# A scan's cost on VectorE, doubled in the planner's model that sets the order of issue

## The chip, the cores and the metric

The kernel runs on one core of a Trainium2 chip. The metric is the device time of one execution in microseconds (us). The core has five engines that take their instructions in order from a queue of their own: TensorE (PE, matrix products), VectorE (DVE), ScalarE (ACT), GpSimd (POOL) and SyncE (SP, which starts most transfers). What one engine hands to another passes through semaphores. An instruction that waits holds up all that stand behind it on its engine.

## The reference, cut to what matters

A trunk of two layers over 512 tokens of width 1024, all in float32. Each layer has a mixer part and a feed-forward part (FFN), with a norm around both:

```python
h = rmsnorm(x, g_pre);  p = h @ W_in        # columns go to four mixers
x = x + rmsnorm(concat(A, B, C, D) @ W_out, g_post)
x = x + rmsnorm(swiglu(rmsnorm(x, ...)), ...)
```

Mixer A is gated linear attention (GLA) in chunks, in both directions over the tokens; B a neighbourhood attention; C a recurrence (RG-LRU) in both directions; D a dilated attention. Two of them hold sums along the tokens:

```python
b = jnp.cumsum(log_a, axis=3)                       # A, in each chunk of 64 tokens
att = einsum(q * exp(b - b_mid), k * exp(b_mid - b))    # A, masked, then att @ v
S = S * d_c[..., None] + kv_c                       # A, a state from chunk to chunk
h = linear_scan(a[0], u[0]) + flip(linear_scan(flip(a[1]), flip(u[1])))    # C
```

The kernel does each of these with one VectorE instruction, `tensor_tensor_scan`, which walks along the free dimension: `y[i] = a[i] * y[i-1] + b[i]`.

## The kernel before, in words

All work is cut into Python generators called threads: a weight to be split, a projection, a direction of a mixer, a head of an attention. Each yields the letter of the engine that its next instructions go to (P, A, V, G for TensorE, ScalarE, VectorE, GpSimd, D for transfers; `A:Exp` also names the table of functions that ScalarE must have loaded). The loop `Builder.go` (L357) runs while the program is built, not on the chip. It keeps a model clock for each engine and takes, again and again, the thread that by the model can start first: `key = (s, th.pri, th.seq)`, where `s` is the later of the engine's clock and the time the thread's input is ready, plus a price for a new table (`SWITCH`, 1290 ns). The order in which the threads are taken is the order of instructions in every engine's queue, and it is fixed from then on.

The model's duration of an instruction comes from `Timed` (L153 on), a wrapper around all four engines: its `call` adds an estimate `t` in ns to `self.b.cost` and then issues the instruction at L198. That is why L198 is the line of nearly every instruction in the profile, and why rows are told apart by tiles. For VectorE (`kind == "V"`) the estimate is 70 ns and 1.04 ns for each element of a row, or 0.52 for some.

`tensor_tensor_scan` has three callers, and there are 24 such instructions, 12 in each layer:

- `dir_a` (L1419), one direction `e` of mixer A for a pair of heads, 4 in a layer: the scan over 512 tokens is the sum of log gates, with a tile `rst` of ones and zeros that restarts it (`m<-rst,m`). ScalarE's exponentials of it follow, then VectorE's products with q and k; then the thread starts `att_a` (L1476), whose matrix products (`bx<-m,m 64*128 64x128`, sixteen for a direction) need these, and `state_a`.
- `gate_c` (L1124), 4 in a layer: the recurrence of mixer C over 512 tokens (`m<-m,m`).
- `state_a` (L1493), 4 in a layer: the state of mixer A over 192 elements.

The first two add 70 to the cost by hand.

Two choices are also made by the model's clocks. `copy` (L412) puts the copy of a PSUM bank on ScalarE or VectorE, whichever clock stands lower. `split` (L403) makes the two parts of an operand: ScalarE rounds it to the high part (`wh`, a CAST), and VectorE or, for most weights, VectorE or GpSimd takes the difference as the low part (`wl`). A dense step of TensorE is the six products of high and low parts into one bank of 128x512.

Of the kernel before, what the change touches and what calls it, by code (L numbers as in the profile page):

```python
# [152 lines left out]
class Timed:  # L153
# [5 lines left out]
    def __getattr__(self, name):  # L159
        f = getattr(self.eng, name)  # L160

        def call(out, *a, **k):
            n = 1
            for s in out.shape[1:]:
                n *= s
            kind = self.kind
            src = a[0] if a and not isinstance(a[0], float) else out
            bank = src.tensor.name[:2] in ("bd", "bx")
            aps = sum(not isinstance(v, (int, float, str)) for v in a[1:] + tuple(k.values()) if hasattr(v, "shape"))
            if kind == "P":  # L170
                if name == "transpose":
                    t = 109.0
                else:
                    m = 1
                    for s in a[0].shape[1:]:
                        m *= s
                    t = max(n / 2.4, m / 1.2) + 13
                    if a[0].dtype == F32:
                        t = max(4 * n / 2.4, 2 * m / 1.2) + 6
                        if a[0].shape[0] == 64 or m == 64:  # L180
                            t *= 0.6
            elif kind == "A":
                t = (51 if bank else 94) + n * 0.833
                if name == "activation" and (aps or "accum_out" in k):
                    t += 93
            elif kind == "V":
                fast = name in ("tensor_scalar", "tensor_copy") and not bank
                t = 70 + n * (0.52 if fast else 1.04)
                if name in ("scalar_tensor_tensor", "tensor_scalar") and aps and n > 16:
                    t += 60  # L190
            elif kind == "G":
                t = 110 + n * (3.4 if name == "tensor_copy" else 2.15)
                if ALU.pow in a:
                    t = 300 + 160 * n
            else:
                t = 60
            self.b.cost += t
            return f(out, *a, **k)  # L198

        return call  # L200
# [1776 lines left out]
```

## Time and profile before

| | us |
|---|---|
| median of 3 runs | 1246.41 (1246.25 to 1246.86) |
| the profiled execution | 1245.09 |
| its span in the trace | 1243.3 |
| TensorE busy | 1203.1 (97%) |
| VectorE busy | 883.8 (71%) |
| ScalarE busy | 707.5 (57%) |
| GpSimd busy | 246.7 (20%) |

The span is the time from the first to the last recorded instruction; 1.8 us of the execution lie outside it. Busy time counts what an engine does, not what it waits. [...] In a timeline, what stands in brackets at the end of a row is the idle time of the engine just ahead of it and the engine and tile that ended it.

### The profile page before, as it was taken

To read this page: it belongs to the slowest core of one execution; us is meant where nothing else is said; L and a number is where in the kernel's file an instruction comes from. 1 tells how busy PE (TensorE), PEld (TensorE's weight loads), DVE (VectorE), ACT (ScalarE), POOL (GpSimd) and SP (SyncE) were. 2 spreads that over 40 slices of the span, in tenths; PEclk is the share of its full clock that TensorE was granted. 3 is DMA by queue.
4 is the path that set the end of the run, shared out by engine and by line. 5 is a ranking of instruction groups with operands and counts; after the bars stand their busy time and mean duration, and the time that the engine had idled before them with its cause. 6 is when DMAs were issued, how large, how long until landed. Compare 5 with 4: busy or idle time off the path is not lost.

```text
span 1243.3 us, 21744 instructions
## 1 busy us (share of the span) xinstructions
PE 1203.1 (97%) x7810; PEld 1050.1 (84%) x7810; DVE 883.8 (71%) x1867; ACT 707.5 (57%) x1604; POOL 246.7 (20%) x255
## 2 busy tenths in 40 slices
PE   7999999999999999999999899999999999999997
PEld 7876777789999999778897677677899999997885
DVE  6467674579766778777875766655897767787775
ACT  6476754565544555566658657455654445556561
POOL 5021111133111110412140111112411121104120
PEclk9999999999999999999999899999999999999999
DMA  7523115218677753988550332430377777639771
GB/s 234 180 75 112 34 61 178 85 45 187 165 187 185 184 138 118 221 227 187 170 199 1 119 85 54 151 110 27 89 191 170 175 193 168 145 92 236 203 182 69
DMA packets 93229, 175.09 MB, mean 141 GB/s; under 512 B 10816, under 2 KB 11200, under 8 KB 93120
## 3 DMA queue, kind: packets, MB, share of 16 engines
q1 hardware_dynamic: 72672, 136.46, 34.6%
q0 software_dynamic: 20160, 36.71, 17.8%
q8 instruction: 61, 1.00, 0.3%
q10 hardware_dynamic: 288, 0.52, 0.1%
q14 instruction: 48, 0.39, 0.1%
HBM read 167.36 MB, written 4.19 MB: 138 GB/s over the span
## 4 chain that ended last, share of the span: by engine, by line
PE 76%; issue 7%; DVE 7%; DMA 4%; ACT 4%; POOL 2%; SPq 0%; POOLq 0%; DVEq 0%; ACTq 0%
PE bx L198 40%; PE bd L198 36%; DVE m L198 5%; ACT m L198 3%; DMA m<-in_wf 3%; POOL wl L198 1%; DMA ws<-in_w 1%; ACT wh L198 1%; DVE wl L198 1%; POOL s L198 1%; POOL m L601 0%; DVE s L198 0%; DMA m<-in_w 0%; POOL att L289 0%; DVE sbd L198 0%
## 5 line engine op out<-in xcount | busy, mean ns | idle before, releaser
L198 PE MATMUL bd<-m,wh 128*128 128x256 f32 (+1 forms) x1600 | 358.5, 318 | 3.4 <-DVE bd L198 2.4
L198 PE MATMUL bx<-m,m 128*128 128x256 f32 (+8 forms) x2096 | 334.0, 340 | 9.7 <-DVE m L198 9.0
L198 DVE TENSOR_TENSOR wl<-m,wh 128x512 fp32r<-128x512 f32 x318 | 219.5, 692 | 152.5 <-ACT wh L198 144.9
L198 DVE TENSOR_TENSOR m<-m,m 128x512 fp32r<-128x512 f32 (+3 forms) x551 | 297.1, 571 | 39.5 <-ACT m L198 37.3
L198 PEld LDWEIGHTS bx<-m,m 128*128 128x128 f32 (+2 forms) x2096 | 257.1, 180 | 70.6 <-issue 25.6
L198 ACT CAST wh<-m 128x512 fp32r<-128x512 f32 x342 | 211.1, 619 | 177.3 <-PE bd L198 90.8
L198 PEld LDWEIGHTS bd<-m,wh 128*128 128x128 f32 x1600 | 261.3, 192 | 25.3 <-issue 6.0
L198 PE MATMUL bd<-m,wl 128*128 128x256 f32 (+1 forms) x800 | 251.6, 314 | 0.0
L198 PEld LDWEIGHTS bd<-m,wl 128*128 128x128 f32 x800 | 153.4, 192 | 9.3
L198 ACT ACTIVATE m<-m 128x256 fp32r<-128x256 f32 (+1 forms) x246 | 112.2, 482 | 61.5 <-DVE m L198 54.9
L198 PE MATMUL bx<-m,wh 128*128 128x256 f32 x768 | 142.4, 284 | 1.0 <-ACT bd L198 1.0
L198 PE MATMUL bd<-m,m 128*128 128x256 f32 (+1 forms) x864 | 137.3, 308 | 1.0 <-DVE m L198 1.0
L514 POOL DMA_DIRECT2D m<-in_wf x76 | 66.9, 973 | 306.2 <-DVE m L198 121.4
L198 PEld LDWEIGHTS bd<-m,m 128*128 128x128 f32 x864 | 119.5, 191 | 8.9 <-DVE m L198 1.4
L198 PEld LDWEIGHTS bx<-m,wh 128*128 128x128 f32 x768 | 119.9, 192 | 1.4 <-ACT bd L198 1.4
L198 ACT CAST m<-m 128x512 fp32r<-128x512 f32 x184 | 108.0, 614 | 15.2 <-DVE m L198 12.7
L198 PE MATMUL bx<-m,wl 128*128 128x256 f32 x384 | 108.8, 283 | 0.0
L198 PE MATMUL bx<-wh,m 128*128 128x512 f32 x296 | 105.7, 398 | 1.6 <-ACT wh L198 1.4
L601 POOL DMA_DIRECT2D m<-in_wf x64 | 56.1, 964 | 165.6 <-DVE m L198 115.2
L198 PE MATMUL bd<-wh,m 128*128 128x512 f32 x232 | 80.7, 394 | 0.0
L198 ACT COPY m<-bx 128x512 f32<-128x512 f32 (+2 forms) x88 | 42.3, 494 | 59.3 <-PE bx L198 58.8
L198 PEld LDWEIGHTS bx<-m,wl 128*128 128x128 f32 x384 | 73.8, 192 | 0.0
(110 smaller groups left out, 1260.7 us busy)
## 6 DMA issues: line engine op xcount, KB each, us to landing
m<-in_wf SPq DMA_DIRECT2D x314, 256.0 KB, 4.0
m<-in_wf POOLq DMA_DIRECT2D x140, 256.0 KB, 5.9
m<-in_w SPq DMA_DIRECT2D x66, 256.0 KB, 5.6
ws<-in_w SPq DMA_DIRECT2D x15, 512.0 KB, 3.8
m<-in_wo SPq DMA_DIRECT2D x24, 256.0 KB, 4.1
m<-in_x SPq DMA_DIRECT2D x14, 256.0 KB, 3.8
m<-in_rpb SPq DMA_DIRECT2D x12, 256.0 KB, 3.6
m<-m SPq DMA_DIRECT2D x32, 64.0 KB, 2.0
```

Of the source, the lines that this page charges most:

```text
L198: return f(out, *a, **k)
L514: self.nc.gpsimd.dma_start(q[name], src, accum_op=ALU.add)
L601: self.nc.gpsimd.dma_start(tile, src, accum_op=ALU.add)
```

## The change

In the model's branch for VectorE, a scan gets its own estimate, 80 ns and 2.08 ns for each element:

```diff
             elif kind == "V":
                 fast = name in ("tensor_scalar", "tensor_copy") and not bank
                 t = 70 + n * (0.52 if fast else 1.04)
+                if name == "tensor_tensor_scan":
+                    t = 80 + n * 2.08
                 if name in ("scalar_tensor_tensor", "tensor_scalar") and aps and n > 16:
                     t += 60
```

With the callers' 70, a scan of 512 counts 1215 ns instead of 672, one of 192 counts 479 instead of 270. No instruction's operands or function change; the planner's choices do. The rows below are the program's order on one engine, by the names of the tiles; the numbers in the names run with the program and shift between the two kernels, and after the change the line of the issue is L200.

TensorE in layer 1, around the first direction of mixer A's first pair. `bd_8062` before is `bd_8060` after, a bank of the projection of v; `m_8102,m_8103` before and `m_8099,m_8100` after are the products of exponentials with k and q; `bd_8293` before and `bd_8265` after are the bank of the projection that follows. Before:

```order
L198 MATMUL bd_8062<-wl_8164,m_6210 128x512
L198 MATMUL bd_8062<-wh_8163,m_6218 128x512
L198 MATMUL bx_8267<-m_8102,m_8103 128x128
L198 MATMUL bx_8268<-m_8102,m_8103 128x128
...
L198 MATMUL bx_8063<-wh_8163,m_6210 128x512
L198 MATMUL bx_8063<-wl_8164,m_6210 128x512
...
L198 MATMUL bd_8293<-m_6203,wh_8188 128x512
```

After:

```order
L200 MATMUL bd_8060<-wl_8163,m_6208 128x512
L200 MATMUL bd_8060<-wh_8162,m_6216 128x512
L200 MATMUL bx_8061<-wh_8162,m_6208 128x512
...
L200 MATMUL bd_8265<-m_6201,wh_8182 128x512
...
L200 MATMUL bx_8283<-m_8099,m_8100 128x128
L200 MATMUL bx_8284<-m_8099,m_8100 128x128
...
L200 MATMUL bd_8265<-m_6203,wh_8182 128x512
```

Two dense steps, one into the bank `bx_8061` and the first into `bd_8265`, stand ahead of the sixteen products of mixer A instead of behind them.

VectorE in the same place: `m_8102<-rst,m_8103` is the scan of direction 0 (a scan prints as SCALAR_TENSOR_TENSOR here), `m_8107<-rst,m_8108` that of direction 1, `m_7963<-m_7964,m_7942` a scan of mixer C, `s_8167` the small products that the exponentials wait for. Before:

```order
L198 SCALAR_TENSOR_TENSOR m_8102<-rst,m_8103 128x512
L198 SCALAR_TENSOR_TENSOR m_8108<-bx_8088,m_8107 128x512
L198 TENSOR_SCALAR s_8167<-m_8102 128x4 x2
L198 TENSOR_TENSOR s_8167<-m_8102 128x4
L198 SCALAR_TENSOR_TENSOR m_8107<-rst,m_8108 128x512
L198 TENSOR_TENSOR m_7942<-m_7955,m_7942 128x512
L198 TENSOR_SCALAR s_8181<-m_8107 128x4 x2
L198 TENSOR_TENSOR s_8181<-m_8107 128x4
L198 SCALAR_TENSOR_TENSOR m_7963<-m_7964,m_7942 128x512
L198 TENSOR_TENSOR m_7938<-m_7938,m_7963 128x512
```

After, where `m_8099<-rst,m_8100`, `m_8104<-rst,m_8105`, `m_7961<-m_7962,m_7940` and `s_8165` are the same things:

```order
L200 SCALAR_TENSOR_TENSOR m_8099<-rst,m_8100 128x512
L200 SCALAR_TENSOR_TENSOR m_8105<-bx_8086,m_8104 128x512
L200 TENSOR_TENSOR m_7940<-m_7953,m_7940 128x512
L200 TENSOR_TENSOR wl_8163<-ws_7604,wh_8162 128x512
L200 SCALAR_TENSOR_TENSOR m_7961<-m_7962,m_7940 128x512
L200 TENSOR_SCALAR s_8165<-m_8099 128x4 x2
L200 TENSOR_TENSOR s_8165<-m_8099 128x4
L200 TENSOR_TENSOR m_7936<-m_7936,m_7961 128x512
L200 TENSOR_TENSOR wl_8183<-m_7670,wh_8182 128x512
L200 TENSOR_TENSOR m_7936<-m_7936,m_7969 128x512
L200 SCALAR_TENSOR_TENSOR m_8104<-rst,m_8105 128x512
```

The scan of direction 1 moved behind the whole of mixer C's scan; a gate product of mixer C, a weight split and mixer C's scan moved ahead of direction 0's small products.

TensorE in layer 0, around the same pair: `m_914,m_915` are direction 0's products, `m_919,m_920` direction 1's, `bd_1137` before and `bd_1131`, `bd_1189` after are banks of a projection. Before:

```order
L198 MATMUL bd_1137<-m_133,wh_1087 128x512
L198 MATMUL bd_1137<-m_125,wl_1088 128x512
L198 MATMUL bx_1189<-m_914,m_915 128x128
L198 MATMUL bx_1190<-m_914,m_915 128x128
...
L198 MATMUL bx_1191<-ident,m_915 128x128 x4
L198 MATMUL bx_1208<-m_919,m_920 128x128
...
L198 MATMUL bx_1217<-ident,m_920 128x128 x4
L198 MATMUL bd_1137<-m_126,wh_1087 128x512
```

After:

```order
L200 MATMUL bd_1131<-m_125,wl_1074 128x512
L200 MATMUL bd_1131<-m_126,wh_1073 128x512
...
L200 MATMUL bd_1189<-m_120,wh_1103 128x512
...
L200 MATMUL bd_1189<-m_121,wl_1104 128x512
L200 MATMUL bx_1212<-m_914,m_915 128x128
L200 MATMUL bx_1213<-m_914,m_915 128x128
...
L200 MATMUL bx_1214<-ident,m_915 128x128 x4
L200 MATMUL bx_1228<-m_919,m_920 128x128
```

Here too the first direction's products stand two dense steps further back.

## Rows read from the trace of the kernel before

**Rows 1.** The page's head: the span, and each engine's busy time.

```profile
span 1243.3 us, 21744 instructions
PE 1203.1 (97%) x7810; PEld 1050.1 (84%) x7810; DVE 883.8 (71%) x1867; ACT 707.5 (57%) x1604; POOL 246.7 (20%) x255
```

**Rows 2.** Waits of TensorE: total us, times, longest.

```profile
PE bx L198 <- DVE m L198: 20.0, 19, 4.8
```

**Rows 3.** Windows: length; busy PE, PEld, DVE, ACT, POOL; granted clock; DMA share; GB/s.

```profile
101.10:103.55 2.45, 0.00 (x1) 0.04 (x1) 2.04 (x4) 2.45 (x8) 0.00 (x0) 1.00 0.11 25
696.20:701.10 4.90, 0.06 (x3) 0.04 (x2) 3.83 (x7) 3.78 (x13) 0.00 (x1) 0.90 0.95 325
701.10:706.90 5.80, 5.80 (x25) 4.81 (x26) 2.53 (x5) 1.90 (x6) 1.57 (x1) 0.50 0.51 191
706.90:765.00 58.10, 58.10 (x347) 43.45 (x347) 35.96 (x83) 36.06 (x75) 9.29 (x6) 1.00 0.23 63
765.00:800.00 35.00, 34.15 (x226) 24.09 (x225) 27.00 (x63) 19.05 (x50) 5.85 (x4) 1.00 0.30 92
```

**Rows 4.** VectorE's groups by shape: busy us, mean ns of one.

```profile
L198 DVE COPY m<-bx 128x512 f32<-128x512 f32 x20 | 13.3, 684 | 7.0 <-PE bx L198 7.0
L198 DVE TENSOR_TENSOR_SCAN m<-rst,m 128x512 f32<-128x512 f32 x8 | 10.7, 1345 | 0.0
L198 DVE TENSOR_TENSOR_SCAN m<-m,m 128x512 f32<-128x512 f32 x8 | 9.5, 1210 | 0.0
L198 DVE TENSOR_TENSOR_SCAN m<-m 128x192 f32<-128x192 f32 x8 | 4.8, 608 | 0.2
```

**Rows 5.** TensorE's timeline in layer 1: start, us, instruction, idle before.

```profile
692.01 0.39 PE L198 MATMUL bd<-wh,m 128*128 128x512 f32 x1
...
693.37 0.39 PE L198 MATMUL bx<-wh,m 128*128 128x512 f32 x1
...
701.09 2.08 PE L198 MATMUL bx<-m,m 64*128 64x128 f32 x16 [4.84 <-DVE m L198]
703.10 0.79 PE L198 MATMUL bx<-wh,m 128*128 128x512 f32 x1
```

**Rows 6.** VectorE's timeline in layer 1.

```profile
683.51 0.66 DVE L198 TENSOR_TENSOR m<-m,m 128x512 f32<-128x512 f32 x1
...
688.62 0.68 DVE L198 TENSOR_TENSOR wl<-ws,wh 128x512 fp32r<-128x512 f32 x1
689.22 1.22 DVE L198 TENSOR_TENSOR_SCAN m<-rst,m 128x512 f32<-128x512 f32 x1
690.36 0.67 DVE L198 SCALAR_TENSOR_TENSOR m<-bx,m 128x512 f32<-128x512 f32 x1
...
692.29 1.72 DVE L198 TENSOR_TENSOR m<-m,m 128x512 f32<-128x512 f32 x1
```

**Rows 7.** ScalarE's timeline in layer 1.

```profile
682.56 0.61 ACT L198 CAST wh<-ws 128x512 fp32r<-128x512 f32 x1
...
686.05 1.28 ACT L198 ACT_TABLE_LOAD   x1
...
690.34 0.63 ACT L198 ACTIVATE m<-m 128x512 f32<-128x512 f32 x1
690.88 0.60 ACT L198 CAST wh<-ws 128x512 fp32r<-128x512 f32 x1
...
698.36 1.86 ACT L198 ACTIVATE m<-m,s 128x128 f32<-128x128 f32 x6
```

**Rows 8.** GpSimd's timeline in layer 1.

```profile
691.56 1.90 POOL L198 TENSOR_TENSOR wl<-ws,wh 128x512 fp32r<-128x512 f32 x1 [11.37 <-ACT wh L198]
```

**Rows 9.** TensorE's timeline in layer 0.

```profile
103.55 1.16 PE L198 MATMUL bx<-m,m 64*128 64x128 f32 x16 [2.47 <-DVE m L198]
...
105.70 1.16 PE L198 MATMUL bx<-m,m 64*128 64x128 f32 x16 [0.40 <-DVE m L198]
```

**Rows 10.** ScalarE's timeline in layer 0.

```profile
93.08 1.28 ACT L198 ACT_TABLE_LOAD   x1
```

## The prediction

> **What bounds the kernel now.** I read the page's head first: TensorE is busy 1203.1 of 1243.3 us, the next engine 883.8 [rows 1]. So an edit to the order of issue can win only where TensorE waits, and the 40 us of idle are all there is. The table of waits comes second: the largest entry is TensorE waiting for a VectorE tile, 20.0 us in 19 waits, the longest 4.8 [rows 2]. The windows around the two longest come third [rows 3]. Before the first direction of the first GLA pair TensorE stands still for 2.45 us in layer 0, and the clock granted around it is 1.00. In layer 1 it stands still for 4.84 us [rows 5] (window: 4.90 long, 0.06 busy), and in the 5.80 us behind that the granted clock is 0.50, the lower of its two levels. TensorE runs there without a pause, but what takes 5.80 us at 0.50 would take 2.90 at 1.00. The wait in layer 1 thus costs 4.84 + 2.90 = 7.7 us, the one in layer 0 only itself.
>
> Both waits have one maker. The intra-chunk products of a direction (call them att) need VectorE's cumulative sum along the tokens (a scan), ScalarE's exponentials of it, and VectorE's products of these with q and k. The scan takes 1.21 to 1.35 us at 512 elements and 0.61 at 192 [rows 4]. The planner before counts 0.67 and 0.27 for these (formula 70 + 1.04 n, plus 70 where the caller adds it), the planner after 1.22 and 0.48. The old model thought att ready about a microsecond too early and put it too early into TensorE's in-order queue, where dense work that is ready stands behind it.
>
> **What the change does.** Nothing is computed otherwise. The rows of the order change on every engine from the first scans on, but on TensorE only in two stretches, each around the mixers of one layer; the dense steps of the FFN keep their order. The totals: three PSUM copies pass from ScalarE to VectorE, two activation-table loads fall away, and some weight splits change between VectorE and GpSimd.
>
> *Layer 1, first pair.* Behind the last dense steps that stand ahead of att in both kernels, the new order puts two more. One step is six matmuls of 128x512; their starts lie 1.36 us apart per step (692.01 and 693.37, six matmuls on) [rows 5]. TensorE ran dry at 696.26 and got att at 701.09, so with two steps more it arrives at 696.1 + 2.72 = 698.8 (I leave out 0.16 for the last product's drain). When is att ready then? I walk the two queues by hand with rows 6 and 7. ScalarE: cast done 683.2, then a table load (1.28), which now stands ahead of the cast that 686.05's load followed; logarithm of direction 0; then a cast that needs VectorE's product, done at 685.4 (three products of 0.60 on from 683.51); cast, logarithm of direction 1, load, square root, two casts, load: 691.3. (A 512-wide operation steps by 0.54, a load takes 1.28.) VectorE: the scan of direction 0 from 687.1 to 688.2, then, moved ahead of the small products that ScalarE's exponentials wait for, a gate product, a weight split and a scan (0.60 + 0.60 + 1.13): small products done at 691.7. Two products and a split follow to 693.5, ScalarE's mixer cast waits for them to 694.2, and then a cast, three pairs of exponentials (0.31 each [rows 7], so 0.6 a pair), three small ones, another cast, the last pair: 698.0. VectorE's last product ends at 699.25. One more price: a GpSimd split of a weight on the same stretch holds up a VectorE product: 1.72 us instead of 0.68 where GpSimd's split at 691.56 ran beside it [rows 6, 8]. The new order also leaves one such split near there, so I add 1.05 once: att ready at 700.4 (bounds 699.4 without, 701.5 with two).
>
> TensorE then waits 700.4 - 698.8 = 1.6 us instead of 4.84. Att starts 0.7 us earlier with 2.72 us more behind it: **3.4 us**. A wait of 1.6 is shorter than layer 0's of 2.45, after which the clock stayed at 1.00 [rows 3], so I take it that it does not fall here either: **2.9 us** more. Bounds: 2.3 (two blocks) to 4.8 for the first term, 0 to 2.9 for the second.
>
> *Layer 0, first pair.* Also two dense steps more ahead of att, so TensorE comes there at 101.1 + 2.7 = 103.8. Att was ready at 103.55 [rows 9]. It comes later now, since one cast more (0.52) stands ahead of the exponentials and the table load of 93.08 [rows 10] now follows the four copies of v, which wait for the end of their dense steps: I add 1.3 and get 104.8. The wait of 2.47 becomes 1.0, and the one of 0.40 before direction 1 [rows 9] goes, because direction 1's chain has had the extra time: **1.9 us** (bounds 0 and 2.9).
>
> *Later in layer 1.* In the stretch of the second pair and the first heads, 765 to 800 us, TensorE idles 35.00 - 34.15 = 0.85 us [rows 3]. Two table loads fewer (1.28 each) fall out of ScalarE's chain just there. I take **0.6** (bounds 0 and 0.85).
>
> *What it gives back.* Three copies of 0.684, all of them among the attention heads of layer 1, move to VectorE [rows 4]; in layer 0 a weight split of 0.6 stands ahead of the last rotary product of the dilated attention; other places of GpSimd's splits mean blocks of 1.05 elsewhere. VectorE has 22 us of idle in the 58 us behind the first pair and 8 in the next 35 [rows 3], which cover most. What comes through hits TensorE as short waits: **-1.5** (bounds 0 and -4, the latter if all three copies and two blocks show).
>
> Sum: 3.4 + 2.9 + 1.9 + 0.6 - 1.5 = 7.3. The profiled execution before took 1245.09 us; the median of the runs, 1246.41, lies 1.32 above it. 1245.09 - 7.3 + 1.32 = 1239.1 us.
>
> [...] In the trace a VectorE product with two SBUF inputs takes 0.68 us alone and 1.72 beside a GpSimd split [rows 6, 8]. [...]
>
> **Rivals.** *More blocks ahead of att in layer 1.* Where the casts land by a few tenths of a microsecond decides whether a second GpSimd split starts first. Att is then ready at 701.5, TensorE waits 2.7 us, and 1.05 of the gain goes: 1240.2. If the clock falls behind that wait as it did behind 4.84, 2.9 more: 1243.1. For it: the block at 692.29 is just such a coincidence. Against: layer 0's wait of about that length left the clock alone.
>
> *The waits only move.* The two dense steps that now stand ahead of att no longer stand behind it, where they covered the products att-times-v. If these become late by as much, TensorE loses behind att what it won before it: near 0, 1246. For it: layer 0's waits before each direction (2.47, then 0.40) show chains with little slack. Against: the copies and masks behind att take some 2 us and most of the projection's dense steps still stand there.
>
> *VectorE becomes the bound (slower).* In layer 1's second half, 765 to 800 us, VectorE is busy 27.0 of 35 [rows 3], and the new order sends it three copies more among the heads (2.05); two more blocks by GpSimd's splits (2.1) would make it 4.15 late. Attention heads need it in bursts, so the average hides this. If TensorE waits for it in one piece there, that is a wait like the 4.84 of layer 1, and it brings the clock down as that one did: 4.15 + 2.9 = 7.05 lost in place of the 1.5. If VectorE is so late, the first pair's att is too: only 2.3 is gained there, and the clock falls. Then 2.3 + 1.9 - 7.05 = -2.85, or 1249.3. It decides once VectorE's 8 us of idle among the heads are no cover, that is once its work there comes in front of a product that TensorE's queue has next.
>
> That the change does nothing is excluded: TensorE's rows move in both layers.
>
> **How the numbers follow.** Forecast with its own spread (1235 to 1241.5): 0.58. More blocks: 0.17, half of it with the clock. Waits only move: 0.14. VectorE the bound: 0.11. The predicted time is the likeliest's, 1239.0. At the best end all terms meet their upper bounds: 4.8 + 2.9 + 2.9 + 0.85 = 11.4, or 1235.0. The range goes from 1234.5 to 1246.5, which takes in the second rival's time and leaves out the slower one and a tail. A measurement of this kernel can tell 0.2%, 2.5 us, from no change: faster means below 1243.9. Forecast and first rival lie below it: 0.75; the second gives 0.14; the third 0.11.
>
> **What would show it.** Right: TensorE's wait before att in layer 1 near 1.6 us with a granted clock near 1.00 behind it; in layer 0 near 1.0 us; dense steps two further in front; TensorE's waits for VectorE tiles near 13 us in sum instead of 20.0. Wrong: a clock of 0.50 anywhere in the mixers of layer 1 (the first term's rival); new waits of a microsecond and more behind att or at the heads in 765 to 800 (second and third); VectorE products of 1.7 us just ahead of att more than once.

## The result and the profile after

| | before | after |
|---|---|---|
| median of 5 runs, us | 1246.41 (1244.19 to 1246.86) | 1232.44 (1231.44 to 1233.09) |
| ratio of after to before, 95% interval | | 0.9895 (0.9885 to 0.9906) |
| the profiled execution, us | 1245.09 | 1232.95 |
| its span, us | 1243.3 | 1231.2 |

The change makes the kernel 14.0 us faster by the medians (1.05% by the ratio) and 12.1 us by the two profiled executions. The forecast was 1239.0 with a range down to 1234.5: the direction is right, the gain about half of what came. Times and ratios here and below are of the fast runs; one run of the kernel with copies done twice (1464.36 us) and one of before (2875.41 us) are left out.

First the page's head and TensorE's largest waits after the change (they answer to [rows 1] and [rows 2]):

```profile
span 1231.2 us, 21747 instructions
PE 1197.8 (97%) x7810; PEld 1047.1 (85%) x7810; DVE 888.0 (72%) x1870; ACT 703.6 (57%) x1599; POOL 243.9 (20%) x255
PE bx L200 <- DVE m L200: 13.5, 14, 1.9
```

The waits for VectorE's tiles fell from 20.0 to 13.5 us, as forecast (near 13). But TensorE's busy time fell too, from 1203.1 to 1197.8, with the same 7810 matmuls. Part of what the page calls busy before was therefore slower work. Of these 5.3 us, 2.9 are the clock behind the wait of layer 1, which my sum had; the rest it did not have.

Next TensorE's timeline after the change, the att of layer 0 and of layer 1 (they answer to [rows 9] and [rows 5]):

```profile
103.42 1.16 PE L200 MATMUL bx<-m,m 64*128 64x128 f32 x16
...
105.10 1.16 PE L200 MATMUL bx<-m,m 64*128 64x128 f32 x16
...
697.41 1.16 PE L200 MATMUL bx<-m,m 64*128 64x128 f32 x16 [1.71 <-DVE m L200]
```

In layer 0 no wait is left before either direction (2.47 and 0.40 before). In layer 1 it is 1.71 (4.84 before), and the group takes 1.16 us in place of 2.08. The windows that answer to [rows 3] (columns as there), the wait of layer 1 first, then three stretches of the same lengths as before:

```profile
695.70:697.41 1.71, 0.01 (x1) 0.03 (x1) 1.57 (x3) 1.71 (x9) 0.00 (x0) 1.00 1.04 397
697.41:703.20 5.79, 5.79 (x54) 4.71 (x56) 3.33 (x7) 4.31 (x11) 1.28 (x1) 1.00 0.07 23
703.20:761.30 58.10, 58.10 (x347) 43.35 (x344) 40.57 (x90) 34.08 (x79) 8.74 (x6) 1.00 0.28 86
761.30:796.30 35.00, 35.00 (x233) 25.60 (x232) 26.73 (x75) 17.42 (x45) 4.20 (x3) 1.00 0.28 89
```

The clock behind the wait (the granted TensorE clock, as a share of full speed) is 1.00 (before: 0.50 from 700.1 to 706.9 us), and TensorE does 54 matmuls in 5.79 us where it did 25 in 5.80 at 0.50 (more of the 54 are small ones). From there to 796 us it does not stand still once.

**Where the time went.** The FFN's matmuls keep their order in all these kernels, so one can compare when TensorE starts the same matmul, by its number in the trace, counted from 0. Each figure is the start in that kernel less the start in the first trace of before, in us. The part of layer 0 is the change from the 400th matmul (68.5 us before) to the 2500th (391.5), the part of layer 1 that from the 4200th (661.8) to the 6000th (958.8).

| kernel | at the 400th | layer 0 | layer 1 |
|---|---|---|---|
| after | 0.04 | -3.17 | -8.83 |
| after, 2nd trace | -0.30 | -3.19 | -8.78 |
| before, 2nd trace | 1.61 | 0.04 | -0.07 |
| before, 3rd trace | 0.99 | 1.11 | 0.38 |
| layer 0 alone | 0.75 | -3.22 | 0.24 |
| layer 1 alone | 0.02 | 0.16 | -8.79 |
| mixer C's scans | -0.68 | -3.45 | -8.29 |
| mixer A's gate scans | -0.62 | -0.20 | -4.99 |
| half of the change | -0.26 | 2.26 | -6.49 |
| twice the change | 0.66 | -1.59 | -10.93 |
| both layers, each its own | 0.20 | -3.17 | -10.94 |
| att alone later | -0.84 | 0.11 | -3.81 |
| one scan more, layer 1 | -0.81 | -3.23 | -5.53 |
| three scans more, layer 1 | -0.20 | -3.19 | -2.14 |
| two scans more, layer 0 | -0.14 | 0.52 | -8.85 |
| copies twice | -0.17 | -3.17 | -6.99 |
| scores later | -0.49 | 0.05 | -0.18 |
| less vector work | 0.67 | 1.17 | -1.13 |
| more vector work | -0.53 | -3.19 | -6.99 |

The first column is what one execution differs from another in its first 37 us, 2.5 us from the earliest to the latest; the medians hold this, and the two other columns do not.

### The profile page after: what moved, and what is told of

Its sections match the earlier page's. It is cut to its first block, busy times and chain, and to the rows that moved or that the text cites. A ratio compares the mean times of both kernels' runs of the same rounds, so it can differ in the third digit from the quotient of the medians.

```text
span 1231.2 us, 21747 instructions
## 1 busy us (share of the span) xinstructions
PE 1197.8 (97%) x7810; PEld 1047.1 (85%) x7810; DVE 888.0 (72%) x1870; ACT 703.6 (57%) x1599; POOL 243.9 (20%) x255
## 4 chain that ended last, share of the span: by engine, by line
PE 84%; DVE 6%; DMA 4%; issue 2%; ACT 2%; POOL 1%; POOLq 0%; SPq 0%; DVEq 0%; ACTq 0%
PE bx L200 44%; PE bd L200 40%; DVE m L200 5%; DMA m<-in_wf 3%; ACT m L200 2%; DVE wl L200 1%; POOL s L200 1%; DMA ws<-in_w 1%; ACT wh L200 0%; DVE s L200 0%; POOL m L603 0%; POOL m L200 0%; POOL wl L200 0%; SPq L393 0%; DVE sbd L200 0%
## 5 line engine op out<-in xcount | busy, mean ns | idle before, releaser
L200 PE MATMUL bd<-m,wh 128*128 128x256 f32 (+1 forms) x1600 | 357.0, 317 | 3.4 <-DVE bd L200 2.4
L200 PE MATMUL bx<-m,m 128*128 128x256 f32 (+8 forms) x2096 | 331.1, 338 | 3.2 <-DVE m L200 2.6
L200 DVE TENSOR_TENSOR m<-m,m 128x512 fp32r<-128x512 f32 (+3 forms) x550 | 296.1, 569 | 46.7 <-ACT m L200 44.6
L200 DVE TENSOR_TENSOR wl<-m,wh 128x512 fp32r<-128x512 f32 x316 | 218.7, 694 | 137.3 <-ACT wh L200 129.2
L200 PEld LDWEIGHTS bx<-m,m 128*128 128x128 f32 (+2 forms) x2096 | 255.2, 178 | 62.2 <-issue 19.5
L200 ACT CAST wh<-m 128x512 fp32r<-128x512 f32 x340 | 209.8, 619 | 167.0 <-PE bd L200 85.4
L200 PEld LDWEIGHTS bd<-m,wh 128*128 128x128 f32 x1600 | 261.1, 192 | 25.0 <-issue 5.9
L200 PE MATMUL bd<-m,wl 128*128 128x256 f32 (+1 forms) x800 | 251.1, 314 | 0.0
L200 PEld LDWEIGHTS bd<-m,wl 128*128 128x128 f32 x800 | 153.0, 191 | 9.3
L200 ACT ACTIVATE m<-m 128x256 fp32r<-128x256 f32 (+1 forms) x246 | 112.2, 483 | 61.6 <-DVE m L200 57.8
L200 PE MATMUL bx<-m,wh 128*128 128x256 f32 x768 | 142.4, 283 | 1.0 <-ACT bd L200 1.0
L200 PE MATMUL bd<-m,m 128*128 128x256 f32 (+1 forms) x864 | 137.2, 307 | 1.0 <-DVE m L200 1.0
L200 PEld LDWEIGHTS bd<-m,m 128*128 128x128 f32 x864 | 119.5, 191 | 8.9 <-DVE m L200 1.4
L200 PEld LDWEIGHTS bx<-m,wh 128*128 128x128 f32 x768 | 119.8, 192 | 1.4 <-ACT bd L200 1.4
L200 ACT CAST m<-m 128x512 fp32r<-128x512 f32 x184 | 108.2, 615 | 10.0 <-DVE m L200 7.5
L200 PE MATMUL bx<-m,wl 128*128 128x256 f32 x384 | 108.7, 283 | 0.0
L200 PE MATMUL bx<-wh,m 128*128 128x512 f32 x296 | 104.5, 394 | 1.7 <-ACT wh L200 1.5
L200 PE MATMUL bd<-wh,m 128*128 128x512 f32 x232 | 80.6, 394 | 0.0
L200 ACT COPY m<-bx 128x512 f32<-128x512 f32 (+2 forms) x85 | 40.9, 491 | 65.1 <-PE bx L200 64.7
L200 PEld LDWEIGHTS bx<-m,wl 128*128 128x128 f32 x384 | 73.7, 192 | 0.0
```

## The experiments

### Which layer, and which scans

With the old estimate the same effect is had by adding 542.48 ns at the callers of the two 512-wide scans and 209.68 at the third. With no condition this gives the order of the changed kernel row for row.

```diff
 dir_a, gate_c:
-        self.cost += 70
+        self.cost += 70 + (542.48 if l == 0 else 0)
 state_a:
+        self.cost += 209.68 if self.lay == 0 else 0
```

> The scans' new estimate holds in layer 0 alone; from layer 1 on the order is that of before. Theory A (each layer's gain is made where its own order moved): TensorE's starts in the FFN of layer 0 lie 3.1 us earlier after the full change, so this one is 3.1 us faster than before, the wait ahead of the first att gone there and the wait of 4.84 in layer 1 with its granted clock of 0.50 unchanged. Rival B (what layer 0 wins is given back at the next wait, as the engines run further ahead): within 1 us of before.

Measured: 1240.63 us, ratio 0.9970 (0.9957 to 0.9982), layer 0 -3.22.

With `l == 1` in place of `l == 0`:

> The new estimate holds in layer 1 alone; layer 0 has the order of before. Theory A: 12.1 - 3.1 = 9.0 us faster than before, with the wait near 1.7 us and a granted clock of 1.00 behind it, and layer 0's waits of 2.47 and 0.40 as before. Rival B: the full gain of 12 to 14 us or close to it, layer 0 giving nothing.

Measured: 1236.79 us, ratio 0.9940 (0.9924 to 0.9955), layer 1 -8.79. Each layer alone gives what it gives in the full change (-3.22 and -8.79 against -3.17 and -8.83), and the other layer moves by 0.24 at most: theory A holds, rival B falls.

With the addition in `gate_c` alone, in both layers:

> Only mixer C's scans (4 in a layer) have the new estimate. The first att of layer 0 stands two dense steps later, as with the full change; that of layer 1 one step later; the second pair of layer 1 stands as before. Theory A: 3 us from layer 0; in layer 1 one step (1.36) of the wait goes, 4.84 to about 3.5, and the clock behind it decides: 4.4 us faster in sum if it falls to 0.50 as before, 7.3 if it stays at 1.00; the loss among mixer D's heads of the second pair stays. Rival E (it is the GLA's own scans whose estimate matters): within 1 us of before.

Measured: 1233.65 us, ratio 0.9906 (0.9891 to 0.9921). Mixer C's scans alone bring -3.45 and -8.29, nearly the whole. Rival E falls, and so does my own number for layer 1: I had reckoned the wait as 4.84 less one dense step. TensorE's timeline of this run, the first att of layer 1:

```profile
694.57 1.16 PE L198 MATMUL bx<-m,m 64*128 64x128 f32 x16 [1.05 <-DVE m L198]
```

The wait is 1.05 although TensorE came only one step later. The order on VectorE and ScalarE had moved as well, and att was ready earlier.

With the addition in `dir_a` alone:

> Only the scans of mixer A's gates (4 in a layer) have the new estimate. The first att of layer 0 stands where it stood before, the four att of layer 1 where the full change has them. Theory A (the place of att in TensorE's queue decides): nothing in layer 0, the 8.8 us of layer 1: 8.8 us faster than before. Rival G (mixer C's scans carry the change, as they alone gave nearly all of it): under 2 us.

Measured: 1239.65 us, ratio 0.9954 (0.9938 to 0.9970): -0.20 and -4.99. Nothing in layer 0, as expected, but only 5.0 of 8.8 in layer 1, though all four att stand in TensorE's queue where the full change has them. The wait was 2.94 and the clock fell behind it:

```profile
698.09:701.03 2.94, 0.00 (x1) 0.03 (x1) 1.66 (x3) 2.94 (x13) 1.26 (x1) 1.00 0.98 372
701.03:703.00 1.97, 1.97 (x18) 1.68 (x19) 1.97 (x4) 1.17 (x4) 0.00 (x0) 0.82 0.05 17
703.00:707.00 4.00, 4.00 (x15) 3.09 (x13) 3.96 (x8) 1.21 (x3) 0.00 (x0) 0.66 0.02 4
```

So the place of att on TensorE is one part, and the order ahead of it on VectorE and ScalarE another: at the same place the wait is 1.2 us longer than after the full change, and the clock costs some 1.7 us.

### The place of att on TensorE alone

The old estimate; in layer 1 the planner takes the first direction of the first pair as ready 2700 ns later:

```diff
 att_a:
+        if self.late_att:
+            self.cur.after = self.start + self.cost + self.late_att
+            self.late_att = 0.0
         b = yield from self.acq("x", 2)
```

> The old estimate, but in layer 1 the first att is held back in the planner so that TensorE issues it two dense steps later, as in the changed kernel; ScalarE, VectorE and GpSimd keep their order of before up to there. Theory A (the place in TensorE's queue makes the first pair's gain): att is ready at 701.1 as before, TensorE gets there at 698.8, waits 2.3 instead of 4.84, the clock stays at 1.00: 2.7 + 2.9 = 5.6 us faster than before; the later loss of layer 1 (some 2.8 us, among the heads of mixer D) stays. Theory A with a falling clock: 2.7 faster. Rival C (the other engines' new order makes att ready earlier, TensorE's place is of no account): within 1 us of before.

Measured: 1240.91 us, ratio 0.9962 (0.9950 to 0.9974), layer 1 -3.81. TensorE's timeline of this run:

```profile
699.79 1.16 PE L198 MATMUL bx<-m,m 64*128 64x128 f32 x16 [2.12 <-DVE m L198]
...
704.38 1.16 PE L198 MATMUL bx<-m,m 64*128 64x128 f32 x14 [1.43 <-DVE m L198]
```

The first wait went from 4.84 to 2.12, as reckoned. Rival C falls: TensorE's place alone has a large effect. But direction 1 now waits 1.43, and behind that the clock falls (0.50 from 705.8 to 709.0 us). By these, 2.72 + 2.9 - 1.43 - 1.7 = 2.5. The starts give less there and more later: 1.65 us are won up to the 4700th matmul (758.4 us before), and 2.15 behind it. I had written off the later loss as untouched; it was not.

### How much of the gain is wait, and how much is clock

The changed kernel, with the first direction's scan repeated on VectorE, not counted by the planner, so that the order of all else is kept:

```diff
 dir_a, after the scan:
+        for _ in range(1 if l == 1 and p == 0 and e == 0 else 0):
+            self.nc.vector.tensor_tensor_scan(ex[:, r], ..., ls[:, r], 0.0, ALU.mult, ALU.add)
```

> The changed kernel, with the first direction's scan of layer 1 done twice in a row (the planner does not count the second one, so that the order of all else is the same): att is ready about 1.13 us later. Theory A (TensorE's wait of 1.71 sits on this chain): the wait becomes 2.8, the kernel 1.1 us slower than the changed one, clock at 1.00 as layer 0's wait of 2.45 left it. Rival F (the chain has slack through ScalarE's casts): under 0.4 us slower.

Measured: 1235.98 us, ratio 0.9930 (0.9914 to 0.9947); layer 1 loses 3.30 against the changed kernel, three times what I expected. The windows of the wait and of what follows:

```profile
694.45:697.83 3.38, 0.00 (x1) 0.03 (x1) 1.90 (x3) 3.38 (x14) 0.00 (x0) 1.00 1.04 390
697.83:699.50 1.67, 1.67 (x17) 1.47 (x18) 1.10 (x2) 1.67 (x5) 0.00 (x0) 0.81 0.11 42
699.50:701.50 2.00, 2.00 (x6) 1.54 (x5) 1.99 (x4) 1.43 (x5) 0.00 (x0) 0.50 0.00 0
701.50:704.00 2.50, 2.50 (x13) 1.80 (x12) 0.13 (x2) 1.42 (x3) 1.29 (x1) 0.84 0.03 7
```

The wait is 3.38, 1.67 more. The clock falls behind it: a mean of 0.81 over 1.67 us, 0.50 over 2.00 and 0.84 over 2.50 is 0.32 + 1.00 + 0.40 = 1.7 us lost. 1.67 + 1.7 = 3.4, against 3.30.

> The same with three scans more: att about 3.4 us later, a wait of 5.1, as long as the one of before. Theory A: 3.4 us slower than the changed kernel by the wait, and 2.9 more because the granted clock falls to 0.50 for some 5.8 us as it did behind 4.84: 6.3 us. If the clock's fall had to do with something else in the old order: 3.4 us only.

Measured: 1240.22 us, ratio 0.9959 (0.9944 to 0.9974); layer 1 loses 6.69. The wait is 5.84 (4.13 more), att takes 2.08 again, and the granted clock is 0.50 behind it to about 706.8 us:

```profile
701.42 2.08 PE L200 MATMUL bx<-m,m 64*128 64x128 f32 x16 [5.84 <-DVE m L200]
```

From 701.42 to 706.8 at 0.50, 2.7 us are lost: 4.13 + 2.7 = 6.8, against 6.69. Theory A holds: the wait and the clock are both on TensorE's path, and the clock follows from the wait, not from anything else in the old order.

In layer 0, with `l == 0` and two scans more:

> The changed kernel, with the first direction's scan of layer 0 done three times in a row, not counted by the planner: att is ready 2.27 us later. In the trace after the change att is ready near 102.9 there and TensorE comes at 103.4, so 0.5 us of slack: theory A gives a wait of 1.8 and 1.8 us lost in layer 0, the clock at 1.00; 4.7 if the clock falls behind it, as it did in layer 0 behind the wait of 2.69 under half of the change.

Measured: 1236.21 us, ratio 0.9926 (0.9911 to 0.9942); layer 0 loses 3.69. The wait is 2.12, and the windows behind it:

```profile
103.30:105.42 2.12, 0.00 (x2) 0.03 (x1) 1.95 (x4) 2.12 (x11) 0.00 (x0) 1.00 0.43 106
105.42:107.00 1.58, 1.58 (x16) 1.40 (x16) 1.06 (x2) 1.29 (x4) 0.70 (x1) 0.64 0.74 275
107.00:109.00 2.00, 2.00 (x14) 1.62 (x14) 1.35 (x3) 0.80 (x2) 0.61 (x1) 0.50 0.29 66
```

2.12 + 1.7 = 3.8. The clock fell behind 2.12 us here and stayed up behind 2.47 in the first trace of before. The length of a wait alone does not tell.

### Half and twice the change

With 271.24 and 104.84 added instead:

> Half of the change: 944 ns at 512 and 375 at 192. First att of layer 0 where it was for direction 0, one step later for direction 1; of layer 1 one step later. Theory A: the wait of layer 1 about 3.5, layer 0's first wait stays near 2.5: 1.4 to 2 us faster if the clock falls as before, 4.3 to 5 if it stays at 1.00. A second look at the same wait as in the run with mixer C's scans alone.

Measured: 1239.82 us, ratio 0.9957 (0.9942 to 0.9971): layer 0 +2.26, layer 1 -6.49. In layer 0 the wait is 2.69, att takes 2.08 behind it as the clock falls, and new waits of 0.67 and 0.39 stand before mixer D's scores. In layer 1 the wait is 1.41, not the 3.5 of the theory: again the other engines' order had moved too.

```profile
103.19 2.08 PE L198 MATMUL bx<-m,m 64*128 64x128 f32 x16 [2.69 <-DVE m L198]
...
699.99 1.16 PE L198 MATMUL bx<-m,m 64*128 64x128 f32 x16 [1.41 <-DVE m L198]
```

With 1084.96 and 419.36 added:

> The scan's estimate raised by the same amount once more, to 1757 ns at 512 and 689 at 192: too high against the measured 1.21 to 1.35 and 0.61. The first att of layer 1 stands five dense steps later than before instead of two. Theory A (a wait at TensorE is what costs, an estimate too high costs little as long as dense work is there): the wait of 1.7 in layer 1 is gone too, 1 to 2 us faster than the changed kernel. Rival D (what stands behind att, its masks, its products with v and the heads, is now late in its turn): slower than the changed kernel by 1 to 5 us, with new waits of TensorE behind att.

Measured: 1233.10 us, ratio 0.9909 (0.9895 to 0.9924): layer 0 -1.59, layer 1 -10.93. Both theories hold in part: in layer 1 the wait is gone and 2.1 us more are won, in layer 0 half of the gain is given back.

Each layer with the estimate that suited it:

> Each layer with the estimate that suited it best in the runs so far: the changed one in layer 0, the one raised twice in layer 1. By the starts of TensorE in the FFN the changed kernel wins 3.2 us in layer 0 and 8.8 in layer 1, the one raised twice 1.6 and about 11. Theory A (the layers' gains add): 14.2 us faster than before at the same point, that is about 2 us or 0.2% faster than the changed kernel. Rival B (the gain of one layer hangs on the state in which the other leaves the queues): as the changed kernel, within 1 us.

Measured: 1231.03 us, ratio 0.9889 (0.9871 to 0.9907): -3.17 and -10.94. Between 690 and 842 us TensorE is busy all but 0.4 us:

```profile
690.00:842.00 152.00, 151.61 (x923) 115.80 (x922) 101.55 (x251) 87.39 (x216) 23.79 (x17) 1.00 0.32 101
```

Theory A holds by the starts of TensorE: 2.1 us better than the changed kernel. By the ratios (0.9889 and 0.9895) the two intervals overlap, so that it beats the changed kernel is read from the trace, and the timed runs do not settle it.

### The second half of layer 1

My prediction charged 1.5 us for copies and splits that move to VectorE. The changed kernel, with each of VectorE's 13 PSUM copies of layer 1 done twice:

```diff
 copy:
             self.dve.tensor_copy(dst, src)
+            if self.lay == 1:
+                self.nc.vector.tensor_copy(dst, src)
```

> The changed kernel, but each of the 13 PSUM copies that VectorE does in layer 1 is done twice, without the planner's knowing: 13 times 0.6 = 7.8 us more for VectorE among the heads of layer 1. My prediction priced 2.05 us of added copies and some blocks at 1.5 us lost, which would make this some 5 us slower than the changed kernel. Theory H (VectorE's idle time covers it; TensorE waited for no VectorE tile there after the change): under 1.5 us slower.

Measured: 1235.11 us, ratio 0.9918 (0.9897 to 0.9939); layer 1 loses 1.84 for 7.8 us of added work, 0.24 for each microsecond. By that rate the three copies that moved (2.05 us) cost 0.5, not 1.5. Theory H is nearer than my price, its bound a little low.

Then the later gain, some 2.8 us of layer 1's 8.83, that I had put at 0.6. The trace of before has a place that I had read too lightly. TensorE's group of twenty scores and products took 3.40 us, and it counts as busy; in the weight loads of the same stretch (770 to 784 us) the waits stand open:

```profile
778.77 3.40 PE L198 MATMUL bx<-m,m 64*128 64x512 f32 x20 [0.33 <-DVE m L198]
PEld bx L198 <- DVE s L198: 1.7, 2, 1.0
PEld bx L198 <- DVE m L198: 1.2, 1, 1.2
```

The twenty are four scores and sixteen small products. The sixteen scores of the second pair of heads, eight, four and four of them before and eight and eight after, fill these windows (columns as in [rows 3]; each runs to the start of the next thing on TensorE), before first:

```profile
776.46:778.77 2.31, 1.98 (x11) 0.68 (x8) 2.26 (x3) 0.59 (x3) 1.32 (x1) 1.00 0.75 188
778.77:781.08 2.31, 2.18 (x5) 0.59 (x5) 2.23 (x7) 0.97 (x3) 0.00 (x0) 1.00 0.43 156
783.64:785.12 1.48, 1.40 (x5) 0.57 (x4) 1.44 (x7) 1.22 (x4) 0.00 (x0) 1.00 0.87 257
```

```profile
772.23:774.15 1.92, 1.92 (x10) 0.69 (x9) 0.76 (x3) 1.24 (x3) 0.00 (x0) 1.00 0.00 0
775.13:777.09 1.96, 1.96 (x9) 0.78 (x8) 1.85 (x10) 1.22 (x4) 1.03 (x1) 1.00 0.00 0
```

They take 6.1 us before and 3.9 after: 2.2 of the 2.8.

Is it the place of those scores? The old estimate, and the scores of the third block held back in the planner so that one dense step goes ahead of them:

```diff
 soft_d:
         b = yield from self.acq("x", 2)
+        if t == 2 and self.cl == (1, 1):
+            self.cur.after = max(self.cur.after, self.start + self.cost + 2000.0)
```

> The old estimate everywhere. In layer 1, second pair of heads of mixer D, the scores of the third block of tokens are held back in the planner so that one dense step and the GLA products stand ahead of them in TensorE's queue. Theory A (VectorE is behind there and frees the PSUM banks late; TensorE stands in front of the scores with ready work behind them): the group of 3.40 us at 778.77 goes, and TensorE's starts in layer 1's FFN lie 2 us earlier than before, the first wait of 4.84 with its clock unchanged. Rival (VectorE's lateness meets the next step in the same way, the softmax behind the scores being just as late): within 0.7 us of before.

Measured: 1245.00 us, ratio 1.0004 (0.9994 to 1.0014); layer 1 -0.18. Theory A falls for the place as tried. The group of 3.40 was gone, but 0.62 now stood before the transposes behind the scores. These are 0.6 of some 2 us; the rest I could not put to single rows (the last four scores took 1.36, but the kernel before has that too, 1.40):

```profile
784.34 0.55 PE L198 MATMUL bx<-ident,m 128*128 128x128 f32 x3 [0.62 <-DVE m L198]
784.82 1.36 PE L198 MATMUL bx<-m,m 64*128 64x512 f32 x4
```

```profile
783.64 1.40 PE L198 MATMUL bx<-m,m 64*128 64x512 f32 x4
```

Is it VectorE, then, which has no pause there? The kernel before without VectorE's two sums of the two directions' att in that pair (the sums' cost stays in the planner, so that the order is kept):

```diff
 mix_a:
         for a in range(2):
             yield "V"
+            if l == 1 and p == 1:
+                am[a] = self.att[a][0]
+                self.cost += 602.48
+                continue
             self.dve.tensor_tensor(am[a], self.att[a][0], self.att[a][1], ALU.add)
```

> The kernel before, without VectorE's two sums of the two directions' att in layer 1's second pair (the products with v take the forward direction's att alone, so the backward direction's part of that pair is left out of the result); every engine's order else is kept. These two took 2.36 us at 776.10, one of them beside a GpSimd split. Theory J (VectorE's backlog from 773 us on is what TensorE waits for in mixer D's heads): TensorE's starts in layer 1's FFN lie about 2 us earlier. Rival (the loss is spread over places that do not hang on VectorE): under 0.7 us.

Measured: 1245.05 us, ratio 0.9994 (0.9984 to 1.0003), with layer 1 at -1.13 and layer 0 at +1.17 (below). Between the two expectations: of 2.36 us that VectorE no longer spent, 1.1 reached TensorE. And the changed kernel, with the same two sums done three times each:

> The changed kernel with the same two sums done three times each, 4 times 0.6 = 2.4 us more for VectorE, not counted by the planner. Theory J (the changed order does this work some 10 us earlier against the heads, where it is covered): under 1 us slower than the changed kernel in layer 1. Rival (VectorE is as tight there as before, and the order only happens to fit): 2 us slower or more.

Measured: 1235.56 us, ratio 0.9915 (0.9900 to 0.9930); layer 1 loses 1.84 for 2.4 us as reckoned, 2.7 by the rows (1.34 and 1.33 from start to start for each added two). TensorE's timeline of this run shows it waiting just where mixer A's products and mixer D's scores stand:

```profile
772.02 0.94 PE L200 MATMUL bx<-m,sbd 128*128 128x128 f32 x6 [0.89 <-DVE sbd L200]
773.57 1.99 PE L200 MATMUL bx<-m,m 64*128 64x512 f32 x8 [0.61 <-DVE m L200]
```

Theory J is half right. VectorE is what TensorE waits for there in the kernel before. It is no less tight after the change: work added at that place costs two thirds of itself. The change also put the second pair's direction 1 two dense steps further ahead on TensorE (758.71 in place of 771.52, though some 9 of these 12.8 us are what the kernel had won by then), and VectorE's two sums for it with it (762.67 and 776.10).

That place is not what most of the gain needs. In the runs with att alone later and with mixer C's scans alone, TensorE's order from the 4634th matmul to the 4829th, direction 1 among them, is that of before; only then does it differ, at the heads, where the scores go eight and eight with a dense step behind the first eight. Both win 2.15 us behind the 4700th matmul; the run with the scores held back wins 0.40 there, the changed kernel some 2.8. The scores' windows of the run with mixer C's scans alone:

```profile
765.84:767.76 1.92, 1.92 (x13) 0.69 (x9) 1.78 (x4) 0.55 (x3) 1.27 (x1) 1.00 0.62 191
772.74:775.24 2.50, 2.50 (x10) 0.97 (x9) 1.58 (x7) 2.39 (x6) 0.00 (x0) 1.00 0.66 211
```

So some 2.2 of the 2.8 us come with the order around the heads, and they come with direction 1 where it was. Which engine's order does it there was not tried: VectorE's and ScalarE's differ from before in these two runs as well.

### What one execution differs from the next

Layer 0 of the run with less vector work has the order of before, and yet lost 1.17 us. Three more traces of the kernels as they are:

> The kernel before, unchanged, a second trace. Theory K (the clock behind the wait of 2.47 in layer 0 is a matter of the single execution): in some of the executions it falls to 0.50 there for a few us, and TensorE's starts behind layer 0 then lie 1.1 to 1.7 us later than in the trace shown ahead of the prediction, apart from the first 37 us. Rival: 1.00 there each time, and what is between the medians and the profiled executions comes from the first stretch alone.

> The kernel before, a third trace; expectations as for the second.

> The changed kernel, unchanged, a second trace. Theory K: the clock is at 1.00 from 60 us to the last FFN of layer 1 save where both kernels have it lower, and TensorE's starts lie as in the first trace of it to within 0.3 us, the first 37 us left out. Rival: it varies as the kernel before does.

Measured: 1246.40, 1246.78 and 1233.73 us. The same wait in the second and in the third trace of before, and two windows of the third:

```profile
105.15 1.16 PE L198 MATMUL bx<-m,m 64*128 64x128 f32 x16 [2.45 <-DVE m L198]
```

```profile
104.54 2.08 PE L198 MATMUL bx<-m,m 64*128 64x128 f32 x16 [2.44 <-DVE m L198]
```

```profile
104.10:106.00 1.90, 1.46 (x14) 1.49 (x16) 1.64 (x4) 1.12 (x4) 0.00 (x0) 0.61 0.45 104
106.00:108.50 2.50, 2.50 (x22) 1.95 (x22) 1.89 (x4) 0.80 (x2) 0.00 (x0) 0.61 0.73 230
```

The same wait, the same order: once att takes 1.16 us, once 2.08 at a lower clock, and layer 0 is 1.11 longer. Theory K holds. Of the eight traces with this wait in layer 0, the clock fell in two. The changed kernel's second trace lies within 0.1 us of its first in both layers.

## Why the prediction was wrong, step by step

The forecast was 1239.0, the median 1232.44: 6.6 us too little gain, and 2.1 below the range. The terms:

| term | forecast | measured |
|---|---|---|
| layer 1, first pair: wait | 3.4 | 4.84 - 1.71 = 3.1 |
| layer 1, first pair: clock | 2.9 | 2.9 |
| layer 0 | 1.9 | 3.2 |
| later in layer 1, with what it gives back | 0.6 - 1.5 = -0.9 | 8.83 - 3.1 - 2.9 = 2.8 |
| the median of after against its profiled execution | +1.32 | 1232.44 - 1232.95 = -0.5 |

The terms of the gain were 7.3 and are 12.0, and the offset differs by 1.8: 6.5 of the 6.6. The largest miss, 3.7, is the later term of layer 1. Behind it stands the premise that an edit of the order can win only where TensorE waits: it gave that term its upper bound of 0.85, and with it a best end of the range that was too slow.

**The first pair of layer 1 was right, by its own steps.** TensorE was to arrive at 698.8 and att to be ready at 700.4. Taken back by the 3.26 us by which TensorE ran earlier there (693.37 before against the same matmul at 690.11 after), it arrived at 695.70 + 3.26 = 698.96, and att started at 697.41 + 3.26 = 700.67. The clock stayed at 1.00, which the second trace and the run of layer 1 alone repeat. The one block by GpSimd that I charged came too (below). But the reason I gave, that a shorter wait than layer 0's 2.45 leaves the clock up, was weaker than I wrote: 2.12 brought it down in one run, and 2.44 did in one trace of the kernel before itself; the number came out right (in all eight traces with a wait of 1.05 to 1.71 there), by a reason that does not hold. I also put the low estimate on the scan in att's own chain. The runs put most of it on mixer C's scans, which share VectorE's queue with it: alone they bring -3.45 and -8.29, mixer A's -0.20 and -4.99.

**The term of layer 0 failed in the walk of ScalarE.** I let the table load's new place delay att by 1.3 us and left a wait of 1.0. VectorE's and ScalarE's timelines after the change show what happened:

```profile
101.39 0.69 DVE L200 TENSOR_TENSOR m<-m,m 128x512 f32<-128x512 f32 x1
102.25 1.90 DVE L200 TENSOR_TENSOR m<-m,m 128x512 f32<-128x512 f32 x3 [0.17 <-ACT m L200]
...
95.00 1.28 ACT L200 ACT_TABLE_LOAD   x1
```

The load is at 95.00 (93.08 before), later as I said. But it is only the exponentials' start; the product that att needs is the first of the three from 102.25, done at 102.9, some 0.5 us earlier than the 103.4 at which the second of these three ended before:

```profile
102.12 1.89 DVE L198 TENSOR_TENSOR m<-m,m 128x512 f32<-128x512 f32 x3
```

ScalarE had less to do between load and last exponential, with the four copies now ahead of the load. I moved one instruction along the chain and did not walk the rest of it, as I had done in layer 1. No wait was left: 2.87 of the 3.2.

**The later term failed twice.** What it gives back was a guess by bounds, and no row was behind the 1.5: TensorE did not stand idle from 697 to 796 us, and 13 copies done twice cost 0.14 us each. And the gain was read from the column of idle time alone (0.85 us in that stretch), when TensorE's busy time also held waits, inside groups and in its weight loads. The group of 3.40 us at 778.77 was in front of me. Of the 2.8, 2.2 lie in the sixteen scores; the other 0.6 stays open.

**The offset was carried over.** I added 1.32 us because the median of before lay so far above its profiled execution. That profiled execution had the clock at 1.00 in layer 0, where others of the same kernel have it fall (1.1 us), and an earlier start than its two other traces (by 1.0 and 1.6 us). After the change the first has no place any more, since that wait is gone. The offset belonged to this kernel's stalls and its executions and was no constant: +1.32 before, -0.5 after.

**The rivals.** More blocks by GpSimd: one came ahead of att, as charged, and not a second. The split at 691.76 held VectorE up at direction 1's small products, 1.36 us where they take 0.21 alone. These are on the way to direction 0's att all the same: ScalarE's queue has direction 1's first exponentials ahead of direction 0's last, and ScalarE stood 1.03 us for them. The chain of what released what, followed back from att, goes this way (last three rows: start, us, what). Without the block att would have been ready about 1.0 us earlier, an estimate from that wait.

```profile
692.09 1.36 DVE L200 TENSOR_SCALAR s<-m 128x4 f32<-128x4 f32 x2
...
691.76 1.59 POOL L200 TENSOR_TENSOR wl<-m,wh 128x512 fp32r<-128x512 f32 x1 [5.61 <-ACT wh L200]
...
693.55 1.28 ACT L200 ACTIVATE m<-m,s 128x128 f32<-128x128 f32 x4 [1.03 <-DVE s L200]
```

```profile
692.09 1.44 DVE s L200 x3
...
693.55 0.15 ACT m L200
...
696.00 1.28 DVE m L200 x2
```

The waits only move: this is what the run with att alone showed (1.43 before direction 1), not the full change, which also moved what direction 1 needs. VectorE becomes the bound: it is tight there, as the run with more of its work shows, but no wait of one piece came, and the order around the heads is better than before. Att's new place on TensorE alone is worth 1.65 us in layer 1 up to the heads, and the order around the heads that came with it 2.15; the new order of the other engines alone was not tried.

## What to carry to other kernels

When a planner sets the order, an estimate that is too low by half a microsecond on one engine can cost ten on another (here 0.54 us for a scan of 512, and 12.1 us by the profiled executions): look for TensorE standing still in front of a group with ready work queued behind it, and compare the estimates with the measured rows for its producers and for what stands ahead of them on their engine (here mixer C's scans mattered most). Read a stage's loss from start to start of the same instruction in two traces, not from idle time, since a wait inside a group of matmuls or ahead of a weight load counts as busy (here in the group of 3.40 us at 778.77). And price a moved instruction by walking its chain to the end each time; what it pushes back may make room for what the consumer needs first.

## What the runs showed of the hardware

**The same wait does and does not bring the clock down.** Behind 2.44 to 2.47 us of idle TensorE in layer 0, with the order ahead of it the same in all but one, the granted clock stayed up in six traces (1.00 in the windows of three of them, the starts of layer 0 within 0.20 us of the first trace of before in all) and fell in two (0.50 over 1.76 us with less vector work, a mean of 0.61 over 1.90 us in the third trace of before), at a price of 1.1 to 1.2 us. Over the waits ahead of a first att in all the runs: up to 1.71 us none was followed by 0.50; single ones of 2.94 and 3.38 were, at about 1.7 us lost, and behind 2.69, 4.84 and 5.84 about 3 us were lost (behind 4.84 and 4.85 in four traces by their rows; in the two other traces of before the starts of layer 1, -0.07 and 0.38, agree). Of two of 2.12, one in layer 0 was, and one in layer 1 (att alone later) was not until a further wait of 1.43 came some 3 us behind it. In these runs a wait that was removed was then worth its length and up to 3 us more, and how much of that varied from one execution to the next.

**VectorE and GpSimd took longer beside each other, once on either side.** The two small products of 128x4 took 1.36 us beside GpSimd's split and 0.21 us alone; and GpSimd's split at 683.37 took 2.78 us where the one at 691.76 took 1.59. In the first it is VectorE that lost, in the second GpSimd: VectorE's scan at 683.84 beside it took 1.22 us, and the one at 690.37 with no split beside it 1.21. What decides which of the two loses, these rows do not show. The three rows:

```profile
683.84 1.22 DVE L200 TENSOR_TENSOR_SCAN m<-rst,m 128x512 f32<-128x512 f32 x1
...
688.36 0.21 DVE L200 TENSOR_SCALAR s<-m 128x4 f32<-128x4 f32 x2
...
683.37 2.78 POOL L200 TENSOR_TENSOR wl<-ws,wh 128x512 fp32r<-128x512 f32 x1 [6.44 <-DVE m L200]
```
